# The PE work of an attention item in one place, and the state-space parameter tiles from an earlier stream by way of DRAM

## The chip, the cores and the metric

One core of one Trainium2 chip. The metric is the device time of one execution, in microseconds (us); lower is better. The engines are called as the profile calls them: PE (TensorE, matrix products and transposes), PEld (its weight loads), DVE (VectorE), ACT (ScalarE), POOL (GpSimd) and SP (SyncE, which here only issues DMAs). "Layer 0" and "layer 1" are the two layers.

## What is computed

A decoder trunk of two layers on 512 tokens of width 1024. In each layer one input projection gives ten column blocks of 512; four mixers work on them, each result is gated, and one output projection adds all four to the residual.

```python
for layer in range(DEPTH):
    proj = rms_norm(x, norm_g[layer]) @ w_in[layer]
    a_u, a_g, qd, kd, vd, b_g, c_x, c_g, m_q, m_g = jnp.split(proj, 10, axis=-1)
    y_a = s5_mixer(a_u, ...)            # A: state-space, 32 groups of 16 channels, 64 complex states
    y_b = diff_attention(q, k, v, lam)  # B: 4 heads, softmax(s1) - lam * softmax(s2), causal
    y_c = rglru_mixer(c_x, ...)         # C: convolution, then a gated linear recurrence
    y_m = memory_attention(m_q, ...)    # M: 4 heads into 256 memory tokens
    mixed = jnp.concatenate([y_a * silu(a_g), y_b * silu(b_g), y_c * silu(c_g), y_m * silu(m_g)], -1)
    x = x + mixed @ w_out[layer]
```

The state-space mixer (S5) builds from `lambda`, `log_dt`, `b` and `c` a decay `abar` and an input matrix `bb`, runs `x_t = abar * x_(t-1) + bb u_t` over the sequence and reads `c` times the state. `abar`, `bb` and all products of them with `b`, `c` and powers of `abar` depend on parameters alone, not on the tokens.

## The kernel before, in words

**Main stream.** A plan (`ORDER`) lists the projection blocks of each layer; layer 0 goes q, v, k, kv (memory keys and values), cx, au, cg, bg, mq, ag, mg, gl (the GLU of the state-space part), then four output blocks (two pairs of groups by two halves of the columns). Layer 1 goes q, k, cx, v, kv, au, mq, bg, mg, ag, cg, gl and the same output blocks. Each block reads weights in pieces of 512 KB (`raw`, 2 buffers, on SP's queue). ACT rounds a piece (`whi`, L166), DVE takes the rest (`wlo`, L172), and three matmuls (hi x hi, hi x lo, lo x hi) replace one fp32 product. `cm_block` (matmuls on L508) and `tm_block` (L528) issue 12 matmuls between two *ticks*. In the au block the stationary tiles are hidden states with a column stride of four (`h_au`).

**Side streams.** Everything else is written as Python generators that the class `Streams` steps once a tick; `yield d` means: go on after d ticks. So at each tick some attention, recurrence (lru), memory or S5 work is traced between the matmuls of the main stream. `D_AT`, `D_S5`, `D_MEM` are those distances. `st.join(name)` ticks until a stream has ended: gl joins S5, the first output block joins S5 and the memory attention, the third the rest.

**Who orders the instructions.** The tile framework takes the traced program and fills each engine's queue: program order is the priority, but an instruction goes only when its inputs and buffers are ready by the framework's own estimate, and work that is ready earlier may run ahead. Buffers of a pool are handed out in program order; most small tiles here come from one pool of nine buffers of 2 KB a partition (`b2`). Each engine's queue and each DMA queue then runs strictly in order on the chip.

**Attention** (L601 on). 16 items a layer: four query blocks i by four heads. `scores(n)` (L638 to L640) issues per map m two score matmuls (fp32r, the query's rounded part and its rest) and one bf16 matmul that adds the causal mask; then DVE and ACT do the softmax (L642 to L654) into `e`. `ptrans(n)` (L662) transposes `e` on PE in i+1 steps and ACT copies it. `av(n)` (L672) multiplies by v in fp32. One turn of the loop issues `scores(n)`, `av(n-2)`, a tick, `ptrans(n-1)`, a tick.

**S5.** `s5_params` (a stream of its own, `s5p`) makes small parameter tiles: `bbx` (input matrix), `cs_` and `cc_` (output matrix), powers `apr`, `api`, and two rotation tables `tab0`, `tab1`. For layer 0 it starts with the kernel, for layer 1 at the third output block of layer 0 (`S5P_AT = 2`). `s5` (L918 on) starts after the au block, when `s5p` has ended. It transposes the input into `U` (L923) and goes through four quarters f of the channels. In each quarter:
- W: two products and a sum on DVE, with two small ACT copies (`bby`, L941), give `wt`; a tick; PE transposes it (L948) into `WT` and multiplies it by `cs_` (L955) for `kq`; eight small POOL DMAs (L966) spread `kq` into `MT`.
- a tick; `B` = `WT` x `U` (L986); DVE makes `VV` (four products on 128x256, and four last steps on 64 partitions each, because the two halves go to different columns), then six steps on 128x512 for the rotation tables `tcq`, `tsq` from `tab0` and `tab1`, then rotates `B` into `xr`.
- a tick; eight scans (L1015), rotation back into `xp`; two ticks; `y` (L1030, L1032) = `MT` x `U` + `VV` x `xp`; a copy; two ticks.

At the end come transposes (L1044) and the GELU (L1046). `tt` (L340) is the DVE helper of all two-operand steps, so their line is L340 whatever they do. `WT`, `VV` and `MT` have one buffer each.

Of the kernel before, what the change touches and what calls it, by code (L numbers as in the profile page):

```python
# [9 lines left out]
F32 = mybir.dt.float32  # L10
# [4 lines left out]
ALU = mybir.AluOpType  # L15
# [34 lines left out]

MEM_AHEAD = 2
BD_AHEAD = 3
S5P_AT = 2
D_MEM = (3, 2, 1)
D_S5 = (1, 1, 1, 2, 2)
D_AT = (1, 1)


class Streams:
# [31 lines left out]
def tile_kernel(ctx: ExitStack, tc: tile.TileContext, A, out):  # L91
# [509 lines left out]
    def attention(l, R):  # L601
# [26 lines left out]
        def scores(n):  # L628
# [8 lines left out]
            for m in range(2):  # L637
                PE.matmul(s[:, m, :M], qh[:, m, h, :], kT[m][:, h, :M], start=True, stop=False)  # L638
                PE.matmul(s[:, m, :M], ql[:, m, h, :], kT[m][:, h, :M], start=False, stop=False)  # L639
                PE.matmul(s[:, m, i * 128:N], idb, cmb, start=False, stop=True)  # L640
            mx = ti(2, "mx")
            V.tensor_reduce(out=mx, in_=s[:, :, :N], op=ALU.max, axis=AX.X)  # L642
# [34 lines left out]
        for n in range(n_it + 2):  # L677
            if n < n_it:
                scores(n)
            if n >= 2:  # L680
                av(n - 2)
            yield D_AT[0]
            if 1 <= n <= n_it:
                ptrans(n - 1)
                yield D_AT[1]

    def attention_fin(l, R):

# [143 lines left out]
    def s5_load(l, R):  # L832
# [7 lines left out]
            nc.sync.dma_start(out=Cw[:, :, i], in_=A[n][l].rearrange("(b g) h p -> (g h) b p", b=4))  # L840
        R["B"], R["Cw"] = B, Cw

    bbx = const.tile([P, 32, 16], F32, tag="bbx", name="bbx")
    cs_ = const.tile([P, 32, 16], F32, tag="cs_", name="cs_")
    cc_ = const.tile([P, 2, 16, 16], F32, tag="cc_", name="cc_")
# [6 lines left out]
    def s5_params(l, R):  # L852
# [37 lines left out]
        for tab, size in ((tab0, 16), (tab1, 8)):  # L890
# [3 lines left out]
            while n < size:  # L894
# [13 lines left out]
                cn, sn_ = c2, s2  # L908
                yield

    def au_evac(au):
        def f(s, a):
            S.copy(au[:, :, :, T - 1 - s, :].rearrange("p q g h -> p (q g) h"), a.rearrange("p (a h) -> p a h", h=16))
        return f

    def s5(l, R):
# [11 lines left out]
        for i in range(2):  # L928
            V.memset(xp[i][:, :, 0], 0.0)
        for f in range(4):  # L930
            qs = slice(4 * f, 4 * f + 4)
            sh = [P, 8, T, 16]
            gs8 = slice(8 * f, 8 * f + 8)
            t1 = b2(sh, "wt1")
            t2 = b2(sh, "wt2")
            tt(t1, bc(apr2[:, gs8], 3, sh), bc(bbx[:, gs8], 2, sh), ALU.mult)

            bby = tiny.tile([P, 8, 16], F32, tag="bby", bufs=1, name=nm("bby"))
            for i in range(2):
                hs, ot = slice(i * 64, i * 64 + 64), slice(64 - i * 64, 128 - i * 64)  # L940
                S.activation(bby[hs], bbx[ot, gs8], AF.Copy, scale=-1.0 if i == 0 else 1.0)  # L941
            tt(t2, bc(api2[:, gs8], 3, sh), bc(bby, 2, sh), ALU.mult)
            tt(t1, t1, t2, ALU.add)
            wd = t1.rearrange("p (q g) d h -> p q (g d h)", g=2)
            yield D_S5[0]
            pt = tp()
            for j in range(4):
# [19 lines left out]
            sh = [P, 4, T, 16]  # L967
            t1 = b2(sh, "wt1")
            t2 = b2(sh, "wt2")

            def cprod(dst, x1, y1, x2, y2, op):
                tt(t1, x1, y1, ALU.mult)
                tt(t2, x2, y2, ALU.mult)
                for g in range(2):
                    hs = slice(g * 64, (g + 1) * 64)
                    tt(dst[hs, :, g], t1[hs], t2[hs], op)

            a_r = bc(apr[:, l, qs, 1:5], 3, sh)
            a_i = bc(api[:, l, qs, 1:5], 3, sh)
            c_r = bc(cc_[:, 0, qs], 2, sh)  # L980
            c_i = bc(cc_[:, 1, qs], 2, sh)
            yield D_S5[1]
            B = sc2((P, 2, 4, NC))
            for j in range(4):
                for i in range(2):
                    PE.matmul(B[:, i, j, :], WT[i][:, j].rearrange("p g c -> p (g c)"), U[:, 4 * f + j, :], start=True, stop=True)  # L986
            cprod(VV[0], a_r, c_r, a_i, c_i, ALU.add)
            cprod(VV[1], a_i, c_r, a_r, c_i, ALU.subtract)

            u1 = b2([P, 4, NC], "u1")  # L990
            u2 = b2([P, 4, NC], "u2")
            tcq = b2([P, 4, NC], "tcq")
            tsq = b2([P, 4, NC], "tsq")
            v4 = [a.rearrange("p q (a b) -> p q a b", b=16) for a in (u1, u2, tcq, tsq)]
            s4 = [P, 4, 8, 16]
            f0 = [bc(tab0[:, i, qs], 2, s4) for i in range(2)]
            f1 = [bc(tab1[:, i, qs], 3, s4) for i in range(2)]
# [104 lines left out]
    for pi, (l, n, u, ids) in enumerate(plan):  # L1102
# [37 lines left out]
        elif n == "au":  # L1140
# [182 lines left out]
```

## Time and profile before

| what | value |
| --- | --- |
| time, median of 3 executions | 924.17 us (922.41 to 924.3) |
| the profiled execution | 923.84 us, of which the span of the trace is 922.1 us |
| PE / PEld / DVE / ACT / POOL busy | 97% / 81% / 71% / 56% / 5% of the span |
| DMA | 90.59 MB, mean 98 GB/s |

The span runs from the first to the last recorded instruction. A busy share is the sum of an engine's instruction times over the span. Matmuls overlap, so a row's mean length of a matmul (0.39 us) is longer than its step in the stream; steps are read from the starts in the timeline. A wait in the trace is put down to whoever signalled last.

### The profile page before, as it was taken

How to read it: one execution, taken by the hardware profiler on the slowest of the kernel's cores; microseconds unless marked ns; L12 is line 12 of the kernel's file. 1: busy time of each engine (PE TensorE's matmuls, PEld its weight loads, DVE VectorE, ACT ScalarE, POOL GpSimd, SP SyncE). 2: the span in 40 equal slices, each digit the busy share in tenths (PEclk: the TensorE clock that was granted, in tenths of full speed). 3: DMA queues.
4: the chain of work that ended last, by engine and by line, in shares of the span. 5: the costliest groups of instructions: out<-in, count | busy, mean ns of one | idle time of the engine just before them, and what ended most of it. 6: DMA issues, size and time to landing. Idle time of an engine off the chain costs nothing.

```text
span 922.1 us, 12510 instructions
## 1 busy us (share of the span) xinstructions
PE 894.3 (97%) x4538; PEld 748.3 (81%) x4538; DVE 655.7 (71%) x1313; ACT 519.1 (56%) x1036; POOL 42.9 (5%) x94
## 2 busy tenths in 40 slices
PE   5999999999999999999999999999999999999997
PEld 4788878987887788888888888798877888788885
DVE  6985877669999946883374675964798998666343
ACT  6674776997333355831454479766646343763123
POOL 1001000001100100000100000000101110000000
PEclk9999999999999999999999999999999999999999
DMA  5833432122122226533343321432121213143322
GB/s 199 204 111 100 141 92 69 47 69 67 55 85 80 63 80 193 137 115 95 111 160 104 91 85 53 147 105 69 50 69 50 74 49 99 62 175 100 98 85 92
DMA packets 81073, 90.59 MB, mean 98 GB/s; under 512 B 23794, under 2 KB 58227, under 8 KB 81011
## 3 DMA queue, kind: packets, MB, share of 16 engines
q1 hardware_dynamic: 77986, 85.98, 30.1%
q10 hardware_dynamic: 720, 2.62, 0.9%
q0 software_dynamic: 2304, 1.18, 0.5%
q8 instruction: 36, 0.59, 0.3%
q14 instruction: 27, 0.21, 0.1%
HBM read 84.92 MB, written 4.19 MB: 97 GB/s over the span
## 4 chain that ended last, share of the span: by engine, by line
PE 70%; DVE 18%; ACT 6%; DMA 3%; issue 2%; SPq 1%; DVEq 0%; ACTq 0%
PE acc L528 36%; PE acc L508 15%; PE acc L1209 5%; DVE u L340 4%; DVE wlo L172 3%; PE tp L1032 2%; DVE xr L1015 2%; PE ms L672 1%; PE tp L826 1%; PE sc L638 1%; ACT whi L166 1%; PE tp L305 1%; PE sc L639 1%; DVE VV L340 1%; PE sc L801 1%
## 5 line engine op out<-in xcount | busy, mean ns | idle before, releaser
L166 ACT CAST whi<-raw 128x1024 fp32r<-128x1024 f32 x136 | 143.3, 1053 | 231.2 <-PE acc L528 119.8
L172 DVE TENSOR_TENSOR wlo<-raw,whi 128x1024 fp32r<-128x1024 f32 x136 | 165.9, 1220 | 115.5 <-ACT whi L166 114.7
L508 PE MATMUL acc<-hThi,whi 128*128 128x512 f32 x384 | 155.0, 404 | 0.0
L508 PE MATMUL acc<-hThi,wlo 128*128 128x512 f32 x384 | 152.8, 398 | 0.0
L508 PE MATMUL acc<-hTlo,whi 128*128 128x512 f32 x384 | 152.2, 396 | 0.0
L528 PE MATMUL acc<-whi,hThi 128*128 128x512 f32 x256 | 105.9, 414 | 0.8 <-ACT whi L166 0.8
L528 PE MATMUL acc<-wlo,hThi 128*128 128x512 f32 x256 | 101.3, 396 | 0.0
L528 PE MATMUL acc<-whi,hTlo 128*128 128x512 f32 x256 | 101.0, 395 | 0.0
L528 PE MATMUL acc<-whi,mxh 128*128 128x512 f32 x256 | 100.1, 391 | 0.0
L528 PE MATMUL acc<-whi,mxl 128*128 128x512 f32 x256 | 100.1, 391 | 0.0
L528 PE MATMUL acc<-wlo,mxh 128*128 128x512 f32 x256 | 100.1, 391 | 0.0
L508 PEld LDWEIGHTS acc<-hThi,wlo 128*128 128x128 f32 x384 | 72.7, 189 | 14.3
L508 PEld LDWEIGHTS acc<-hThi,whi 128*128 128x128 f32 x384 | 72.7, 189 | 12.9
L508 PEld LDWEIGHTS acc<-hTlo,whi 128*128 128x128 f32 x384 | 72.7, 189 | 12.9
L528 PEld LDWEIGHTS acc<-whi,hThi 128*128 128x128 f32 x256 | 56.3, 220 | 8.9 <-ACT whi L166 1.2
L528 PEld LDWEIGHTS acc<-whi,hTlo 128*128 128x128 f32 x256 | 56.1, 219 | 7.9 <-DVE hTlo L308 0.2
L528 PEld LDWEIGHTS acc<-wlo,hThi 128*128 128x128 f32 x256 | 56.7, 221 | 7.1
L528 PEld LDWEIGHTS acc<-whi,mxh 128*128 128x128 f32 x256 | 48.1, 188 | 9.8
L528 PEld LDWEIGHTS acc<-whi,mxl 128*128 128x128 f32 x256 | 48.1, 188 | 9.8
L528 PEld LDWEIGHTS acc<-wlo,mxh 128*128 128x128 f32 x256 | 48.1, 188 | 9.6
L966 POOL DMA_DIRECT2D MT<-kq x64 | 32.1, 509 | 367.8 <-DVE kq L340 230.3
L648 ACT ACTIVATE e<-sc,nmx 128x128 f32<-128x128 f32 (+3 forms) x64 | 33.3, 530 | 11.7 <-DVE nmx L644 10.2
(305 smaller groups left out, 1664.6 us busy)
## 6 DMA issues: line engine op xcount, KB each, us to landing
raw<-in_w_in_dram SPq DMA_DIRECT2D x80, 512.0 KB, 3.6
raw<-in_w_out_dram SPq DMA_DIRECT2D x32, 512.0 KB, 3.3
raw<-in_w_mem_kv_dram SPq DMA_DIRECT2D x16, 512.0 KB, 3.4
x<-in_x_dram SPq DMA_DIRECT2D x8, 512.0 KB, 5.2
raw<-in_s_w_glu_dram SPq DMA_DIRECT2D x16, 256.0 KB, 2.9
mt<-in_mem_dram SPq DMA_DIRECT2D x4, 512.0 KB
xd<-x SPq DMA_DIRECT2D x4, 512.0 KB, 4.3
x<-xd SPq DMA_DIRECT2D x4, 512.0 KB, 6.8
```

The lines of the kernel that those rows point to most:

```text
L166: S.copy(hi, wbuf[j])
L172: V.tensor_tensor(out=lo, in0=raw, in1=hi, op=ALU.subtract)
L305: lastins["pe"] = PE.transpose(pt[:, k, :], h[:, kk * 128:(kk + 1) * 128], ident)
L340: V.tensor_tensor(out=o, in0=a, in1=b, op=op)
L508: PE.matmul(a[j][:, :ncol], w[:, kk, c], h(k), start=(hf == 0 and i == 0), stop=(hf == 1 and i == 3 * nh - 1))
L528: PE.matmul(a[t], h(k, t), w[:, kk, :], start=(p == 0 and kk == 0 and i == 0), stop=(p == np_ - 1 and kk == 1 and i == 2))
L638: PE.matmul(s[:, m, :M], qh[:, m, h, :], kT[m][:, h, :M], start=True, stop=False)
L648: S.activation(e[:, m, :N], s[:, m, :N], AF.Exp, bias=nmx[:, m:m + 1], scale=0.125, accum_out=sm[:, m:m + 1])
L966: G.dma_start(out=MT[g * 64 + 64 - n:g * 64 + 64, g, t], in_=kq[g * 64:g * 64 + n])
L1015: V.tensor_tensor_scan(out=xr_[i][:, j, :], data0=dec, data1=xr_[i][:, j, :], initial=0.0, op0=ALU.mult, op1=ALU.add)
L1032: PE.matmul(y[:, j, :], xp[i][:, j, :], VV[i][:, j].rearrange("p g t h -> p (g t h)"), start=False, stop=(i == 1))
L1209: PE.matmul(a, w[:, k, s, j * 128:(j + 1) * 128], h[:, 2 * hf + k, :], start=(hf == 0 and i == 0), stop=(hf == 1 and i == 5))
```

## The change

Five edits. (1) In `scores`, both maps' score matmuls come first, then both mask matmuls. (2) A turn of the attention's loop issues `scores(n)`, `ptrans(n-1)`, `av(n-2)` one behind the other, then two ticks. (3) The W, VV and table products move from `s5` to the end of `s5_params`, each result written to DRAM by a DMA on SP, twelve steps three ticks apart. (4) `s5` reads them back: W and the two tables by SP, VV by four POOL DMAs a quarter into the two partition halves; it starts after au as soon as the first quarter is there. (5) `s5p` of layer 1 starts at the first output block of layer 0.

```diff
-S5P_AT = 2
+S5P_AT = 0
 D_S5 = (1, 1, 1, 2, 2)
-D_AT = (1, 1)
+D_S5P = 3
+D_AT = 2
...
             for m in range(2):
                 PE.matmul(s[:, m, :M], qh[:, m, h, :], kT[m][:, h, :M], start=True, stop=False)
                 PE.matmul(s[:, m, :M], ql[:, m, h, :], kT[m][:, h, :M], start=False, stop=False)
+            for m in range(2):
                 PE.matmul(s[:, m, i * 128:N], idb, cmb, start=False, stop=True)
...
             if n < n_it:
                 scores(n)
+            if 1 <= n <= n_it:
+                ptrans(n - 1)
             if n >= 2:
                 av(n - 2)
-            yield D_AT[0]
-            if 1 <= n <= n_it:
-                ptrans(n - 1)
-                yield D_AT[1]
+            yield D_AT
...
+    s5dram = ctx.enter_context(tc.tile_pool(name="s5dram", bufs=2, space=bass.MemoryType.DRAM))
...
+        R["s5d"] = []
+        for f in range(4):
+            d = {n: s5dram.tile([P, 512], F32, tag=f"{n}{f}", name=nm(f"{n}d")) for n in ("wd", "vv", "tc", "ts")}
+            w1 = b2(sh, "wp1")
+            w2 = b2(sh, "wp2")
+            tt(w1, bc(apr2[:, gs8], 3, sh), bc(bbx[:, gs8], 2, sh), ALU.mult)
...
+            tt(w2, bc(api2[:, gs8], 3, sh), bc(bby, 2, sh), ALU.mult)
+            tt(w1, w1, w2, ALU.add)
+            nc.sync.dma_start(out=d["wd"], in_=w1.rearrange("p g d h -> p (g d h)"))
+            yield D_S5P
...
+            for i, (x1, x2, op) in enumerate(((a_r, a_i, ALU.add), (a_i, a_r, ALU.subtract))):
+                tt(v1[:, i], x1, c_r, ALU.mult)
+                tt(v2[:, i], x2, c_i, ALU.mult)
+                tt(v1[:, i], v1[:, i], v2[:, i], op)
+            nc.sync.dma_start(out=d["vv"], in_=v1.rearrange("p i q t h -> p (i q t h)"))
+            yield D_S5P
...
+            for n, (i, j), (i2, j2), op in (("tc", (0, 0), (1, 1), ALU.subtract), ("ts", (1, 0), (0, 1), ALU.add)):
+                a1 = b2(s4, "tp1")
+                a2 = b2(s4, "tp2")
+                tt(a1, f0[i], f1[j], ALU.mult)
+                tt(a2, f0[i2], f1[j2], ALU.mult)
+                tt(a1, a1, a2, op)
+                nc.sync.dma_start(out=d[n], in_=a1.rearrange("p q a b -> p (q a b)"))
+            R["s5d"].append(d)
+            yield D_S5P
...
         for f in range(4):
+            while len(R["s5d"]) <= f:
+                yield
...
-            tt(t1, bc(apr2[:, gs8], 3, sh), bc(bbx[:, gs8], 2, sh), ALU.mult)
...
-            tt(t2, bc(api2[:, gs8], 3, sh), bc(bby, 2, sh), ALU.mult)
-            tt(t1, t1, t2, ALU.add)
-            wd = t1.rearrange("p (q g) d h -> p q (g d h)", g=2)
+            d = R["s5d"][f]
+            wd = b2([P, 4, 128], "wd")
+            nc.sync.dma_start(out=wd.rearrange("p q c -> p (q c)"), in_=d["wd"])
             yield D_S5[0]
...
+            vd = d["vv"].rearrange("p (i q c) -> p i q c", i=2, q=4)
+            for i in range(2):
                 for g in range(2):
                     hs = slice(g * 64, (g + 1) * 64)
-                    tt(dst[hs, :, g], t1[hs], t2[hs], op)
...
+                    G.dma_start(out=VV[i][hs, :, g].rearrange("p q t h -> p q (t h)"), in_=vd[hs, i])
+            tcq = b2([P, 4, NC], "tcq")
+            tsq = b2([P, 4, NC], "tsq")
+            nc.sync.dma_start(out=tcq.rearrange("p q c -> p (q c)"), in_=d["tc"])
+            nc.sync.dma_start(out=tsq.rearrange("p q c -> p (q c)"), in_=d["ts"])
             yield D_S5[1]
...
-            cprod(VV[0], a_r, c_r, a_i, c_i, ALU.add)
-            cprod(VV[1], a_i, c_r, a_r, c_i, ALU.subtract)
...
-            tt(v4[0], f0[0], f1[0], ALU.mult)
-            tt(v4[1], f0[1], f1[1], ALU.mult)
-            tt(v4[2], v4[0], v4[1], ALU.subtract)
-            tt(v4[0], f0[1], f1[0], ALU.mult)
-            tt(v4[1], f0[0], f1[1], ALU.mult)
-            tt(v4[3], v4[0], v4[1], ALU.add)
...
             def s5_all(l=l, R=R):
-                while "s5p" in st.live:
+                while "s5d" not in R:
                     yield
```

## Rows read from the trace of the kernel before

**Rows 1.** The page, part 1: busy time, share of the span, instructions.

```profile
PE 894.3 (97%) x4538; PEld 748.3 (81%) x4538; DVE 655.7 (71%) x1313; ACT 519.1 (56%) x1036; POOL 42.9 (5%) x94
```

**Rows 2.** Windows: stretch, length, busy PE, PEld, DVE, ACT, POOL, granted clock, DMA.

```profile
88.00:214.00 126.00, 125.36 (x684) 106.30 (x683) 94.75 (x173) 104.93 (x227) 3.47 (x9) 1.00 0.27 81
214.00:342.00 128.00, 123.06 (x648) 103.42 (x647) 113.39 (x210) 54.08 (x98) 16.05 (x32) 0.99 0.24 75
364.00:571.00 207.00, 206.64 (x981) 170.74 (x980) 128.89 (x246) 114.08 (x198) 3.93 (x10) 1.00 0.37 110
662.00:802.00 140.00, 137.23 (x757) 114.00 (x756) 120.19 (x221) 69.24 (x147) 13.96 (x28) 1.00 0.21 67
```

**Rows 3.** PE's waits, 214 to 342, then 662 to 802: total us, times, longest.

```profile
PE tp L1032 <- DVE xp L340: 1.7, 3, 0.8
PE tp L1044 <- ACT yf L1046: 1.7, 1, 1.7
PE tp L948 <- DVE wt L340: 1.5, 1, 1.5
...
PE tp L699 <- DVE bg L700: 1.2, 1, 1.2
PE tp L1032 <- DVE xp L340: 0.6, 1, 0.6
PE tp L826 <- ACT yf L1046: 0.4, 1, 0.4
PE tp L819 <- ACT yf L1046: 0.3, 1, 0.3
```

**Rows 4.** Windows around the wait at L948, columns as in rows 2.

```profile
213.50:217.00 3.50, 2.01 (x17) 1.60 (x16) 3.50 (x5) 3.25 (x9) 0.00 (x0) 0.99 0.31 109
217.00:221.00 4.00, 4.00 (x13) 3.24 (x13) 3.85 (x11) 2.63 (x5) 3.04 (x7) 0.58 0.45 137
```

**Rows 5.** Timeline of PE, one item's scores and masks: start, length, line, tiles.

```profile
159.46 0.34 PE L638 MATMUL sc<-kT,qh 128*128 128x384 f32 x1
159.63 0.34 PE L639 MATMUL sc<-kT,ql 128*128 128x384 f32 x1
159.81 0.23 PE L640 MATMUL sc<-cmb,idb 128*128 128x128 bf16 x1
159.85 0.42 PE L638 MATMUL sc<-kT,qh 128*128 128x384 f32 x1
160.11 0.33 PE L639 MATMUL sc<-kT,ql 128*128 128x384 f32 x1
```

**Rows 6.** Timeline of PE, one item's transposes in the au block.

```profile
154.66 0.49 PE L662 MATMUL tp<-cst,e 128*128 128x128 f32 x3
154.91 0.60 PE L528 MATMUL acc<-whi,hThi 128*128 128x512 f32 x1
155.35 0.40 PE L528 MATMUL acc<-wlo,hThi 128*128 128x512 f32 x1
155.59 0.40 PE L528 MATMUL acc<-whi,hTlo 128*128 128x512 f32 x1
```

**Rows 7.** Line L340 on DVE: ns min/median/max, first and last start.

```profile
L340 DVE TENSOR_TENSOR u<-tab,tab x32: 675/685/695, 219.3 to 760.1; 128x512 f32<-128x512 f32 x32
L340 DVE TENSOR_TENSOR VV<-wt,wt x32: 406/418/423, 219.9 to 757.3; 64x256 f32<-64x256 f32 x32
```

**Rows 8.** DMA issues: engine, count, KB each, median us to landing.

```profile
raw<-in_s_w_glu_dram SPq DMA_DIRECT2D x16, 256.0 KB, 2.9
...
bd<-in_lru_w_a_dram POOLq DMA_DIRECT2D x4, 64.0 KB, 2.3
```

**Rows 9.** Waits of SP's queue, 214 to 342: total us, times, longest.

```profile
SPq L152 <- DVE wlo L172: 93.1, 13, 11.2
```

**Rows 10.** Instructions that write or read bbx: ns, first and last start.

```profile
L941 ACT ACTIVATE bby<-bbx x16: 308/308/311, 50.3 to 720.6; 64x128 f32<-64x128 f32 x16
L340 DVE TENSOR_TENSOR wt<-apr,bbx x8: 672/678/689, 212.7 to 746.6; 128x512 f32<-128x512 f32 x8
```

More of the change, by code (lines that the diff above doesn't have):

```diff
@@ L909, in s5_params @@
                 yield
+        R["s5d"] = []
+        for f in range(4):
+            qs, gs8 = slice(4 * f, 4 * f + 4), slice(8 * f, 8 * f + 8)
+            d = {n: s5dram.tile([P, 512], F32, tag=f"{n}{f}", name=nm(f"{n}d")) for n in ("wd", "vv", "tc", "ts")}
+            sh = [P, 8, T, 16]
+            w1 = b2(sh, "wp1")
+            w2 = b2(sh, "wp2")
+            tt(w1, bc(apr2[:, gs8], 3, sh), bc(bbx[:, gs8], 2, sh), ALU.mult)
+            bby = tiny.tile([P, 8, 16], F32, tag="bby", bufs=1, name=nm("bby"))
+            for i in range(2):
+                hs, ot = slice(i * 64, i * 64 + 64), slice(64 - i * 64, 128 - i * 64)
+                S.activation(bby[hs], bbx[ot, gs8], AF.Copy, scale=-1.0 if i == 0 else 1.0)
+            tt(w2, bc(api2[:, gs8], 3, sh), bc(bby, 2, sh), ALU.mult)
+            tt(w1, w1, w2, ALU.add)
+            nc.sync.dma_start(out=d["wd"], in_=w1.rearrange("p g d h -> p (g d h)"))
+            yield D_S5P
+            sh = [P, 4, T, 16]
+            a_r = bc(apr[:, l, qs, 1:5], 3, sh)
+            a_i = bc(api[:, l, qs, 1:5], 3, sh)
+            c_r = bc(cc_[:, 0, qs], 2, sh)
+            c_i = bc(cc_[:, 1, qs], 2, sh)
+            v1 = b2([P, 2, 4, T, 16], "vp1")
+            v2 = b2([P, 2, 4, T, 16], "vp2")
+            for i, (x1, x2, op) in enumerate(((a_r, a_i, ALU.add), (a_i, a_r, ALU.subtract))):
[4 more added lines that the diff above has]
+            yield D_S5P
+            s4 = [P, 4, 8, 16]
+            f0 = [bc(tab0[:, i, qs], 2, s4) for i in range(2)]
+            f1 = [bc(tab1[:, i, qs], 3, s4) for i in range(2)]
+            for n, (i, j), (i2, j2), op in (("tc", (0, 0), (1, 1), ALU.subtract), ("ts", (1, 0), (0, 1), ALU.add)):
[7 more added lines that the diff above has]
+            yield D_S5P
     def au_evac(au):
@@ L930, in s5 @@
         for f in range(4):
+            while len(R["s5d"]) <= f:
+                yield
             qs = slice(4 * f, 4 * f + 4)
[L932 to L935, printed above, removed]
-            tt(t1, bc(apr2[:, gs8], 3, sh), bc(bbx[:, gs8], 2, sh), ALU.mult)
[L938 to L941, printed above, removed]
-            tt(t2, bc(api2[:, gs8], 3, sh), bc(bby, 2, sh), ALU.mult)
-            tt(t1, t1, t2, ALU.add)
-            wd = t1.rearrange("p (q g) d h -> p q (g d h)", g=2)
+            d = R["s5d"][f]
+            wd = b2([P, 4, 128], "wd")
+            nc.sync.dma_start(out=wd.rearrange("p q c -> p (q c)"), in_=d["wd"])
             yield D_S5[0]
@@ L966, in s5 @@
                     G.dma_start(out=MT[g * 64 + 64 - n:g * 64 + 64, g, t], in_=kq[g * 64:g * 64 + n])
[L967 to L973, printed above, removed]
+            vd = d["vv"].rearrange("p (i q c) -> p i q c", i=2, q=4)
+            for i in range(2):
                 for g in range(2):
                     hs = slice(g * 64, (g + 1) * 64)
-                    tt(dst[hs, :, g], t1[hs], t2[hs], op)
[L978 to L981, printed above, removed]
+                    G.dma_start(out=VV[i][hs, :, g].rearrange("p q t h -> p q (t h)"), in_=vd[hs, i])
[3 more added lines that the diff above has]
+            nc.sync.dma_start(out=tsq.rearrange("p q c -> p (q c)"), in_=d["ts"])
             yield D_S5[1]
@@ L986, in s5 @@
                     PE.matmul(B[:, i, j, :], WT[i][:, j].rearrange("p g c -> p (g c)"), U[:, 4 * f + j, :], start=True, stop=True)
-            cprod(VV[0], a_r, c_r, a_i, c_i, ALU.add)
-            cprod(VV[1], a_i, c_r, a_r, c_i, ALU.subtract)
             u1 = b2([P, 4, NC], "u1")
             u2 = b2([P, 4, NC], "u2")
[L992 to L997, printed above, removed]
-            tt(v4[0], f0[0], f1[0], ALU.mult)
-            tt(v4[1], f0[1], f1[1], ALU.mult)
-            tt(v4[2], v4[0], v4[1], ALU.subtract)
-            tt(v4[0], f0[1], f1[0], ALU.mult)
-            tt(v4[1], f0[0], f1[1], ALU.mult)
-            tt(v4[3], v4[0], v4[1], ALU.add)
             xr_ = [b2([P, 4, NC], f"xr{i}") for i in range(2)]
```

## The prediction

> **What bounds the kernel now.** I read the page first: TensorE (PE) is busy 97% of the span, VectorE (DVE) 71% [rows 1]. So the time is PE's work plus the time in which PE has none or works at a worse pace; DVE counts only where PE waits for it. The change leaves every matmul in, so all it can win are those losses. The windows view then shows where they are [rows 2]. In each row compare the stretch with PE's busy time, then look at DVE. While the attention of layer 0 runs (88 to 214 us), DVE is busy 94.75 of 126 us (75%) and PE lacks 0.64 us. While the state-space (S5) part of layer 0 runs (214 to 342), DVE is at 113.39 of 128 (89%) and PE lacks 4.94. In layer 1 (662 to 802) it is 120.19 of 140 (86%) and 2.77. From the last projections of layer 0 to the start of the next attention (364 to 571) DVE is at 62% and PE lacks 0.36.
>
> The waits view of the two S5 stretches names what PE waited for [rows 3]: the W tiles from DVE (1.5 us, L948), the decayed states xp from DVE (1.7, and 0.6 in layer 1), the gate bg from DVE (1.2), and the GELU on ScalarE (1.7). The first costs more than its length: PE is busy 2.01 of 3.5 us around it, and in the next 4 us the granted clock is 0.58, a mix of the full level, 2.4 GHz, and the half, 1.2 [rows 4]. That loses 4 x 0.42 = 1.7 us more.
>
> The last loss shows only in starts. A mask matmul (bf16) is followed by the other map's first score matmul: this takes from 159.85 to 160.11, 0.26 us, where the first map's took 0.17 from 159.46 [rows 5]. After the three transposes of an item, the next projection matmul holds PE from 154.91 to 155.35, 0.44 us, the one after it 0.24 [rows 6].
>
> **The change, part by part.**
> *Masks together.* Both masks follow both maps' scores, so a mask stands ahead of a score once less per item. A score after a mask lost 0.26 - 0.17 = 0.09 us; the mask's own slot is short, 0.04 [rows 5], so I count 0.07 net. 32 items: -2.2 us, between 0 (the scheduler pulls them apart) and -2.9 (0.09 each).
>
> *Transposes and AV behind the scores.* The 32 transpose groups lose a place of their own, and so an exit into the projection stream. One exit holds 0.20 us over the pace [rows 6], but the three transposes before it took only 0.25 (154.66 to 154.91), so part of it is their own unfinished work: I take 0.12, between the mask's 0.07 and 0.20. This exit is in the au block, whose stationary tiles are strided; I count the eight items that fall there, -1.0 us, between 0 and 32 x 0.20 = -6.4, nearer 0 because most groups stand elsewhere. Each item still takes two ticks, so the pace of the attention stays. Its transposes come one tick sooner after their scores (two, not three): where the softmax is late, the scheduler puts other matmuls between, and the grouping is lost there rather than PE.
>
> The Trainium skill has a rule against this part ("TensorE: Matmul & The Clock Gate", step-by-step section): weight loads are pulled ahead of matmuls in flight, so the next tile's load hides behind this one's matmul. Here the slot of 0.44 us after transposes against 0.24 [rows 6] says that this fails at a change of kind; by the rule the term would be zero, the third rival below.
>
> *Parameter tiles out of the S5 stretch.* Per quarter of the channels DVE did three steps for W at 0.69 us (the length of a step on a whole tile), four half-partition writes at 0.418 for VV and four products on as many elements a partition, so as long, and six steps of 0.69 for the tables [rows 7]: 2.1 + 3.3 + 4.1 = 9.5 us, 38 per layer. Without them DVE's load is 113.39 - 38 = 75 of 128 us in layer 0 and 82 of 140 in layer 1, both 59%, under the 75% of the attention's stretch, where PE lacked 0.5%. At that rate PE lacks 0.005 x 268 = 1.3 us. The GELU waits stay, 1.7 and about 0.7 in layer 1, since ScalarE makes them. So 7.7 - 1.3 - 2.4 = 4.0 us of idle time go, and the half clock with the L948 wait, 1.7: -5.7 us. Ends: 0, if the loads come as late as the products did, and -7.7 - 1.7 = -9.4.
>
> *What takes its place.* The same tiles are made once in the parameter stream, 3 + 6 + 6 products a quarter (VV's last step is now whole, so six at 0.418): 2.1 + 2.5 + 4.1 = 8.7 us, 35 per layer, with the two small ScalarE copies. Layer 1's stream starts at the first output block, in the stretch at 62%: (128.89 + 35) of 207 is 79% [rows 2], which I price at 0.5 us, between 0 and 2.5 (the layer boundary, with norm and transposes, lies in it). In layer 0 there is no such room: the steps ahead take 23 ticks and q, v and k have 24, so the twelve new steps of three ticks begin with the attention (88 us) and end some seven ticks after au, whose last tick, the 52nd, is near 214 us. So the attention's stretch holds up to 94.75 + 35 = 130 us of DVE in 126. Some spills into the S5 stretch, which now has room. PE there would lack between the 0.5% of now and the 3.9% of 214 to 342, so +0 to +4.3, and up to 1.7 of half clock: I take +1.5, nearer the low end because mostly projections fill PE there, and the attention's result is needed only by the third output block.
>
> *DMAs and queues.* Each quarter adds four writes and three reads of 256 KB on SP and four reads of 64 KB on POOL. The 256 KB loads of now land in 2.9 us, the 64 KB POOL loads of bd in 2.3 [rows 8]. The writes are read much later. VV on POOL stands behind eight small MT issues; its matmuls come four ticks on, and a tick is 12 matmuls at 0.24, 2.9 us [rows 6]: even one after another, 4 x 2.3 = 9.2 us, the loads fit in 11.6. W and the tables on SP are asked for one tick ahead of their use, just the landing time. And SP's queue is in order and sits waiting nearly always: 93.1 us in 13 waits for wlo in the S5 stretch of layer 0 [rows 9]. A load behind one comes late, and a weight load behind a write that waits for DVE does too; the latter is covered by the two spare weight pieces (24 matmuls each, 11 us in all). Price of new waits: +0.7, between 0 and the slower rival's 9.6.
>
> **Sum** against the profiled execution, 923.84 us (span 922.1): -2.2 - 1.0 - 5.7 + 0.5 + 1.5 + 0.7 = -6.2, so 917.6. That execution lies 0.3 under the median of 924.17, so I forecast 918.0 for the median. A measurement of this kernel can tell about 0.2%, 1.8 us.
>
> **The rivals.**
> 1. *Moved, not removed.* Layer 0's DVE is overfull during the attention and costs there what the S5 stretch gives back: +4.3 + 1.7 in place of +1.5, so 922.5, on the edge of no change. For it: 130 us in 126. Against: the S5 stretch at 89% lost PE time through its own short chain, which the attention has not.
> 2. *Slower: W's load comes too late.* L948 waits for the SP load as it did for DVE at 214 us. Each such case costs 1.5 + 1.7 = 3.2 us [rows 3, 4]; against a forecast 6.2 under, it decides from three of the eight quarters on; with three it gives 918.0 - 0.7 + 9.6 = 926.9. For it: SP waits 93.1 of 128 us. Against: the load is ready to go as soon as a buffer is free, and the scheduler lets ready work run ahead: the first bby copy runs at 50.3 us, its product only at 212.7 [rows 10].
> 3. *No grouping.* The scheduler parts the work again, or weights do load ahead: 918.0 + 3.2 = 921.2.
> 4. *More.* The GELU tail comes sooner and its waits go (-2.4), layer 0 has room (-1.5), half the exits beyond my eight save 0.12 (-1.4): 912.7.
>
> **How the numbers follow.** Forecast 0.43 (own range 914 to 921), rival 1 0.18, rival 2 0.15, rival 3 0.11, rival 4 0.13. Faster by over 0.2% (under 922.3) are the forecast, rivals 3 and 4 and under half of rival 1: 0.75. Within 0.2%: the rest of rival 1, 0.10. Slower (over 926.0): rival 2, 0.15. The range of 8 in 10 goes from 911.5, a little under rival 4, to 927.0, which takes in rival 2 at three quarters and leaves out more of them.
>
> **What would show it.** Right: DVE under 65% in both S5 stretches; no wait before the W transposes (L948 of before) and no dip of the clock after it; hardly a wait for xp; two masks next to each other with starts 0.04 to 0.06 us apart, then transposes and AV; 88 to 214 us over 90% DVE with PE lacking under 2 us. Wrong: the W transposes waiting for the load of wd, DVE waiting for tcq or tsq, POOL's VV releasing the y matmuls, weight casts waiting for raw loads, or the PE time of 88 to 214 us growing by what the S5 stretch sheds.

## The result: slower, and the profile after

The changed kernel takes 933.86 us (median of four runs, 930.73 to 934.83), the kernel before in the same session 923.57 (922.41 to 924.30): a ratio of 1.0111, 95% interval 1.0095 to 1.0127. I had forecast 918.0. The profiled execution is one of 934.83 us with a span of 932.9.

The page, part 1, of the changed kernel (busy time, share of the span, instructions; against [rows 1]):

```profile
PE 895.9 (96%) x4538; PEld 751.8 (81%) x4538; DVE 647.2 (69%) x1297; ACT 520.0 (56%) x1036; POOL 62.8 (7%) x126
```

The totals explain nothing. TensorE (PE) has the same matmuls and is busy 1.6 us more, VectorE (DVE) even has 8.5 us less to do; the span grew by 10.8. So PE lost time in gaps, and the question is where. The windows view, with the four stretches cut at the same projection matmuls as in [rows 2] (length, then busy PE, PEld, DVE, ACT, POOL, granted clock, DMA):

```profile
88.00:224.60 136.60, 127.74 (x676) 108.56 (x675) 117.89 (x225) 108.32 (x237) 6.40 (x14) 0.96 0.32 102
224.60:352.60 128.00, 123.81 (x655) 104.00 (x654) 84.02 (x149) 51.25 (x89) 23.57 (x44) 0.99 0.36 111
374.70:581.50 206.80, 206.33 (x980) 170.83 (x979) 155.99 (x306) 116.39 (x204) 6.38 (x14) 1.00 0.43 131
672.60:813.50 140.90, 137.58 (x763) 115.14 (x761) 91.32 (x160) 69.97 (x150) 20.50 (x38) 1.00 0.28 89
```

Read the first number after each colon pair, the length, against [rows 2]: 126 became 136.6, 128 stayed 128.0, 207 became 206.8, 140 became 140.9. **The whole loss lies in layer 0's attention**, 10.6 us, and the state-space (S5) stretches gained next to nothing, though DVE's share there fell from 89% to 66% and from 86% to 65%. (The border between these two stretches is good to 1 us: the attention's last AV, eight matmuls, stands before it in the kernel before and behind it in all others whose stretches are compared here. The two together grew by 10.6.) The load went where I said it would go, and the time did not follow it. In the first row DVE is busy 118 of 137 us: 86%, less than I had feared, and yet PE lacks 8.9 us and the clock is at 0.96.

PE's waits in 88 to 228, in the S5 part of layer 0 (228 to 356) and in 672 to 813 (total us, times, longest; against [rows 3]):

```profile
PE sc L639 <- ACT e L650: 5.5, 2, 4.2
PE sc L640 <- DVE ql L341: 1.7, 1, 1.7
...
PE tp L1049 <- DVE xp L341: 3.8, 4, 1.9
PE tp L985 <- DMA wd<-wdd: 0.4, 1, 0.4
...
PE tp L1049 <- DVE xp L341: 2.1, 3, 1.1
```

New are the scores that wait for an exp (they need the score buffer that the exp still reads) and for ql. In S5 the waits for the W tile (L948 of before) and for the gate went, as I had counted on, and so did the GELU wait of layer 0, which I hadn't; but the waits for xp grew from 1.7 to 3.8 us and from 0.6 to 2.1. (Part of both is the attention's edits: e1 below has neither the W wait nor the gate's, and waits 2.3 and 1.6 us for xp.) Around the long wait for the exp, two windows of the same columns:

```profile
189.50:194.00 4.50, 0.42 (x4) 0.23 (x3) 3.04 (x6) 4.43 (x12) 0.00 (x0) 0.77 0.13 48
194.00:198.00 4.00, 3.92 (x15) 3.21 (x16) 2.77 (x5) 4.00 (x8) 0.00 (x0) 0.50 0.03 11
```

PE stands for 4.2 us, and in the four that follow the granted clock is 0.50, its half level of 1.2 GHz: some 2 us more. ScalarE (ACT) is full here (4.43 of 4.50). The scores that this exp belongs to were issued at 184.8 to 188.5 us; before the change the same item's ran at 170.1 to 172.4. So the attention came 14.7 us later and 40 projection matmuls further down the stream (620 of them stand before these scores, 580 before the change), into the stretch where ACT has the recurrence's sigmoids. What put it behind stands at 106 to 119 us. ACT's timeline there (start, length, line, tiles):

```profile
106.35 0.37 ACT L675 ACTIVATE qT<-ms,rc 128x128 f32<-128x128 f32 x1
...
112.24 0.62 ACT L624 CAST qh<-qT 64x512 fp32r<-64x512 f32 x1
112.89 2.01 ACT L167 CAST whi<-raw 128x1024 fp32r<-128x1024 f32 x2
114.79 0.26 ACT L666 COPY pT<-tp 128x128 f32<-128x128 f32 x1
114.95 0.37 ACT L677 ACTIVATE jk<-ms,rc 128x128 f32<-128x128 f32 x1
```

The first row is the evacuation of an AV, the last the square of the same AV, which could follow at once and comes 8.6 us later. The pT in between copies transposes that PE made at 105.6. And DVE's timeline just beside it:

```profile
111.67 1.88 DVE L341 TENSOR_TENSOR tp<-tab,tab 128x512 f32<-128x512 f32 x3
113.48 0.68 DVE L341 TENSOR_TENSOR tp<-tp,tp 128x512 f32<-128x512 f32 x1
...
116.12 0.16 DVE L653 RECIPROCAL rc<-sm 128x2 f32<-128x2 f32 x1
```

The softmax of the third item had its exps by 106.4 us; its reciprocal comes at 116.1, behind table products ("tp" here is the product of L341, not the PSUM tile). Two theories fit. The products fill DVE and stand ahead of the softmax; or the products take buffers that pT and the square need, so that the order of the queues puts these late, and with them the reciprocal: its result `rc` has two buffers, and the square of two items before must first free one. A third showed in SP's queue, 88 to 228 us:

```profile
SPq L153 <- DVE wlo L173: 47.2, 13, 7.2
SPq L952 <- DVE tp L341: 28.4, 6, 13.3
SPq L928 <- DVE wp L341: 18.9, 2, 13.5
```

The writes to DRAM wait up to 13.5 us for their product, with weight loads queued behind them.

One prediction is seen at once. PE's timeline of one item's last score and both masks, against [rows 5]:

```profile
106.98 0.28 PE L640 MATMUL sc<-kT,ql 128*128 128x256 f32 x1
107.10 0.29 PE L642 MATMUL sc<-cmb,idb 128*128 128x128 bf16 x2
107.19 0.48 PE L529 MATMUL acc<-whi,mhi 128*128 128x512 f32 x1
```

Both masks are over in 0.09 us, and no score follows a mask any more.

### The profile page after: what moved, and what is told of

The parts are those of the page before. It is cut to its first block, busy times and chain, and to the rows that moved or that the text cites. A ratio compares the mean times of both kernels' runs of the same rounds, so it can differ in the third digit from the quotient of the medians.

```text
span 932.9 us, 12684 instructions
## 1 busy us (share of the span) xinstructions
PE 895.9 (96%) x4538; PEld 751.8 (81%) x4538; DVE 647.2 (69%) x1297; ACT 520.0 (56%) x1036; POOL 62.8 (7%) x126
## 4 chain that ended last, share of the span: by engine, by line
PE 67%; DVE 16%; ACT 6%; DMA 5%; issue 4%; POOL 1%; SPq 1%; DVEq 0%; ACTq 0%; POOLq 0%
PE acc L529 33%; PE acc L509 16%; PE acc L1226 5%; DVE wlo L173 2%; DVE u L341 2%; DVE xr L1032 2%; PE tp L1049 2%; ACT whi L167 1%; DMA MT<-kq 1%; PE sc L802 1%; PE tp L827 1%; DVE tp L341 1%; PE ms L674 1%; PE tp L306 1%; PE sc L639 1%
## 5 line engine op out<-in xcount | busy, mean ns | idle before, releaser
L529 PE MATMUL acc<-whi,hThi 128*128 128x512 f32 x256 | 104.0, 406 | 0.8 <-ACT whi L167 0.8
L509 PEld LDWEIGHTS acc<-hThi,whi 128*128 128x128 f32 x384 | 72.8, 189 | 13.5 <-ACT whi L167 0.4
```

Of the source, the lines that this page charges most:

```text
L509: PE.matmul(a[j][:, :ncol], w[:, kk, c], h(k), start=(hf == 0 and i == 0), stop=(hf == 1 and i == 3 * nh - 1))
L529: PE.matmul(a[t], h(k, t), w[:, kk, :], start=(p == 0 and kk == 0 and i == 0), stop=(p == np_ - 1 and kk == 1 and i == 2))
```

## The experiments

The theories: **A**, DVE overfull (my rival 1); **B**, weight loads behind waiting writes on SP; **C**, the attention's own new order; **D**, the pool b2 of nine 2 KB buffers runs out. Ratios are against the kernel before on the same chip; between runs on different chips a difference in us is good to about 1, as the kernel before itself had medians from 922.95 to 923.98.

**The two halves apart.** e1 is the kernel before with the attention's edits, e2 the changed kernel without them, e3 the kernel before with the first of them alone, e4 the changed kernel with the square's tile moved:

```
-                PE.matmul(s[:, m, i * 128:N], idb, cmb, start=False, stop=True)      # e1, e3; undone in e2
+            for m in range(2):
+                PE.matmul(s[:, m, i * 128:N], idb, cmb, start=False, stop=True)
...
+            if 1 <= n <= n_it:                       # e1; undone in e2
+                ptrans(n - 1)
             if n >= 2:
                 av(n - 2)
-            yield D_AT[0]
-            if 1 <= n <= n_it:
-                ptrans(n - 1)
-                yield D_AT[1]
+            yield D_AT
...
-            jk = b2([P, 128], "jk")                  # e4
+            jk = tiny.tile([P, 128], F32, tag="ajk", name=nm("jk"))
```

> The kernel before with the attention's two edits alone (masks behind both maps' scores; transposes and AV behind the scores); the state-space part makes its own tiles as before. Kernel before 923.6, changed 933.9. Theory A (VectorE is overfull during layer 0's attention), theory B (weight loads stand behind writes that wait for VectorE on SP) and theory D (the nine b2 buffers run out because of the new products) all need the products in the attention, so they expect no loss here: 919 to 923, my -3.2 of the prediction. Theory C (the new order of the attention itself stalls TensorE, since scores, transposes and AV stand in a row with nothing between) expects most of the loss here: 929 or more, with scores that wait for the exp around 190 us.

Measured 920.92 us, ratio 0.9973 (0.9962 to 0.9985). Faster; theory C, taken by itself, falls.

> The changed kernel with the attention's emission as before (mask after each map's scores, transposes a tick after the scores); parameter tiles by way of DRAM as in the change. Theories A, B and D expect the loss to stay: 931 to 937 (the changed 933.9 plus the 0 to 3 that the attention's edits had saved). Theory C expects it to go: 918 to 925.

Measured 927.46, ratio 1.0042 (1.0027 to 1.0057). The way over DRAM alone loses 4 us, not 10: less than A, B or D had said. The halves (-2.4 and +4.2) make +1.8, the whole +10.3; 8.5 us are interaction: the new order costs nothing by itself, but with the products in the attention it does.

> The kernel before with the masks behind both maps' scores and nothing else. My step of -2.2 expects 921.4 (between 920.7 and 923.6). If the mask's place between the maps costs nothing that a later start doesn't cost too, 923.6 within 0.5. All of A to D expect no loss; a loss over 1 would put part of it on the masks.

Measured 921.90, ratio 0.9986 (0.9976 to 0.9995): -1.4, so the mask's place does cost something, if less than I had it.

> The changed kernel with the square of the attention's AV (only its sum is used) written to a small tile of its own and no longer to one of the nine b2 buffers. Theory D expects the softmax chain no longer to wait for a b2 buffer: 925 to 929, at least 5 of the 10 us given back, and the attention to finish its items earlier than in the changed kernel. Theories A, B and C expect 933 within 1.5.

Measured 929.16, ratio 1.0063 (1.0048 to 1.0078). A junk tile of 512 bytes a partition taken out of b2 gives back 4.7 us. That speaks for D, and its timeline shows how (ACT):

```profile
106.48 0.37 ACT L675 ACTIVATE qT<-ms,rc 128x128 f32<-128x128 f32 x1
106.73 0.38 ACT L677 ACTIVATE jk<-ms,rc 128x128 f32<-128x128 f32 x1
...
115.07 0.41 ACT L666 COPY pT<-tp 128x128 f32<-128x128 f32 x2
```

The square now follows its AV at once. pT, which still needs a b2 buffer, is as late as before. Two windows of the changed kernel, then of e4, show that the loss has two places and which of them came back:

```profile
110.00:132.00 22.00, 18.49 (x80) 13.68 (x79) 20.25 (x40) 13.59 (x36) 0.00 (x0) 0.92 0.44 142
176.00:198.00 22.00, 17.72 (x82) 15.33 (x82) 15.41 (x26) 21.74 (x39) 0.00 (x0) 0.86 0.10 37
...
110.00:132.00 22.00, 18.41 (x82) 13.94 (x82) 20.26 (x39) 13.56 (x36) 0.00 (x0) 0.92 0.46 151
176.00:198.00 22.00, 20.46 (x100) 17.52 (x100) 15.64 (x28) 21.44 (x46) 0.00 (x0) 1.00 0.22 70
```

At 110 to 132 us PE lacks 3.5 us in the one and 3.6 in the other; at 176 to 198 it lacks 4.3 in the changed kernel, with the granted clock at 0.86, and 1.5 in e4 at 1.00. e2, with the old order, has the same two figures at 3.0 and 0.6, and its pT too comes late (116.23 us, behind two weight casts). So the first loss goes with the late pT; the second, the long wait for the exp, came only where the new order and the square in b2 met. Why the new order needs more of b2 isn't shown.

**One suspect each.** e5 keeps the way over DRAM for layer 1 only:

```
         R["s5d"] = []
+        if l == 0:
+            return
...
+            own = l == 0
+            if own:
...
```

(where "own" is set, the S5 part makes its tiles as before). e6 sends layer 0's products to POOL, e7 sends the writes from POOL's queue, e8 changes the S5 part's pauses (the edits in short):

```
-                tt(w1, ...)                          # e6, all products of s5_params
+                (G if l == 0 else V).tensor_tensor(out=w1, ...)
-            nc.sync.dma_start(out=d["wd"], ...)      # e7, all four writes
+            G.dma_start(out=d["wd"], ...)
-D_S5 = (1, 1, 1, 2, 2)                               # e8
+D_S5 = (1, 1, 1, 3, 1)
```

> The changed kernel with the way over DRAM in layer 1 only; layer 0 makes its tiles in its state-space part as before; the attention's edits stay. The loss was found in layer 0's attention, so this should come out under the kernel before: 919 to 922, that is the 920.9 of the attention's edits alone, less what layer 1's state-space stretch gains (0 to 1.5) plus up to 1 for the products in the output blocks. If layer 1 loses something too, 923 or more. The prediction's step of -5.7 for both layers would make it about 918.

Measured 920.07, ratio 0.9968 (0.9955 to 0.9981). Layer 1 loses nothing; what it gains over e1 (0.9 us by the times, 0.5 by the ratios) is inside the intervals.

> The changed kernel with layer 0's products (15 a quarter) computed by POOL in place of VectorE; same buffers, same writes to DRAM, same order of the streams. Theory A (VectorE overfull, the products stand ahead of ql, of rc and of the W casts) expects most of the loss to go: 921 to 926. Theory D (b2 buffers run out) expects it to stay or grow, since a slower engine holds the buffers longer: 933 to 940. Theory B (weight loads behind waiting writes on SP) expects the same, as the writes wait longer still: 933 to 940.

Measured 937.32, ratio 1.0151 (1.0134 to 1.0168). With DVE rid of the products the loss grew, as D and B had it and A not. This isn't clean: POOL and DVE slow each other (last section). PE's waits over the span show the attention as the victim again:

```profile
PE tp L664 <- DVE e L656: 5.2, 6, 1.8
PE sc L639 <- ACT e L650: 3.2, 5, 1.9
```

> The changed kernel with the sixteen writes a layer issued from POOL's queue in place of SP's. Theory B expects weight loads no longer to stand behind writes that wait for VectorE: 926 to 930, with raw pieces 29 to 31 issued in an even rhythm around 190 us. Theories A and D expect 932 to 935, no difference that counts.

Measured 934.56, ratio 1.0126 (1.0111 to 1.0141): no gain. PE's two largest waits in 88 to 228 us are those of the changed kernel, to the digit (5.5 in 2 for the exp, 1.7 for ql). Theory B falls.

> The changed kernel with the state-space part's y matmuls three ticks (not two) after the scans, and the next quarter's load one tick (not two) after them, so that a quarter stays eight ticks. The waits for xp (5.9 us in 7 in the changed kernel, 2.3 in 4 before) did not go with VectorE's load. If they are the length of the chain from B to xp against three ticks of cover, they go: 928 to 931. If VectorE's load or the loads of tcq and tsq make them, or if the wait only moves to W, 933 within 1.5.

Measured 930.85, ratio 1.0085 (1.0070 to 1.0100): 3.0 less than the changed kernel, as expected. (A quarter is seven ticks in both, not eight as I wrote.)

**The pool itself.** e9 leaves all of the change in place and only moves the product tiles out of b2, into one of the fourteen 8 KB buffers; e10 does the opposite to e1, with no products in the attention:

```
-            w1 = b2(sh, "wp1")                       # e9; v1, v2, a1, a2 alike
-            w2 = b2(sh, "wp2")
+            pb = b8([P, 4, 512], "pp")
+            w1, w2 = (pb[:, k].rearrange("p (g d h) -> p g d h", g=8, d=T) for k in range(2))
...
-    sm2 = ctx.enter_context(tc.tile_pool(name="sm2", bufs=9))      # e10
+    sm2 = ctx.enter_context(tc.tile_pool(name="sm2", bufs=8))
```

e11 is e5, and e12 is e9, each with the pauses of e8.

> The changed kernel with the products of a quarter in one 8 KB tile of the pool of fourteen large buffers, so that none of the six product tiles takes one of the nine b2 buffers; VectorE's work, the writes and the streams stay. Theory D (b2 runs out: pT and the AV's square get their buffer late, so softmax chain and attention fall behind) expects 922 to 927, with the pT copy of the second item near 110 us in place of 114.8 and the scores of item i3 h0 near 172 us in place of 184.8. Theory A (VectorE overfull) expects 932 to 935. If the large buffers run out in their turn, the S5 part or the gates wait for one instead: above 928 with a wait for them.

Measured 921.90, ratio 0.9982 (0.9972 to 0.9992): 12 us less than the changed kernel, and faster than the kernel before. The windows of the four stretches, cut as above, then ACT's timeline:

```profile
88.20:215.10 126.90, 123.54 (x676) 106.06 (x675) 115.18 (x219) 105.48 (x234) 3.80 (x11) 1.00 0.32 104
215.10:339.80 124.70, 122.03 (x656) 102.71 (x655) 79.35 (x140) 50.79 (x88) 23.63 (x44) 1.00 0.34 111
361.80:568.90 207.10, 206.75 (x980) 170.65 (x980) 157.16 (x306) 116.14 (x204) 6.37 (x14) 1.00 0.42 131
659.70:800.00 140.30, 137.46 (x762) 115.06 (x761) 91.32 (x160) 69.92 (x150) 20.57 (x38) 1.00 0.28 89
```

```profile
111.40 0.27 ACT L666 COPY pT<-tp 128x128 f32<-128x128 f32 x1
111.57 0.37 ACT L677 ACTIVATE jk<-ms,rc 128x128 f32<-128x128 f32 x1
...
113.34 1.99 ACT L167 CAST whi<-raw 128x1024 fp32r<-128x1024 f32 x2
```

The attention's stretch fell from 136.6 to 126.9 us with nearly as much for DVE to do in it: DVE is busy 91% of it, more densely than the 86% of the slower kernel, and PE lacks 3.4 where it lacked 8.9. What differs is the order: pT stands ahead of the weight casts again. The item at 184.8 us now has its scores at 176.9 (I had said 172). Theory D is shown in this: with the same work for every engine, the place of the product tiles makes the loss; A is not its cause. (The one large tile also makes the products of a quarter wait for each other in another way than eight small ones did; e4, which leaves the products alone, speaks for the pool by itself.)

> The attention's edits alone (920.9) with eight b2 buffers in place of nine and no products in the attention at all. Theory D expects that the pool alone makes a loss: 924 or more, in the stretch of 88 to 214 us. Theory A expects at most 1: 921 to 922.

Measured 931.26, ratio 1.0084 (1.0069 to 1.0100). One buffer less costs 10.3 us over e1, without one product in the attention: the pool is at its limit already. But the loss isn't where I said. Cut at the same matmuls, 88 to 214 stays at 123.7 us, the S5 stretch of layer 0 takes 130.1 (e1: 126.5), the start of layer 1's attention, 571 to 662 in the kernel before, 95.1 (e1: 91.3), and the S5 stretch of layer 1 142.8 (e1: 140.7). The first two, whole:

```profile
212.40:342.50 130.10, 122.80 (x658) 102.97 (x656) 112.09 (x208) 54.23 (x102) 16.10 (x32) 1.00 0.23 72
571.70:666.80 95.10, 90.89 (x504) 80.23 (x503) 64.68 (x120) 64.22 (x155) 3.47 (x7) 0.96 0.28 87
```

> The best so far (DRAM in layer 1 only, attention's edits; 920.1) with the y matmuls one tick later. In the changed kernel that saved 3.0, in both state-space parts. The chain from B to xp is the same in both ways of making the tiles, so 916.5 to 918.5; if the waits for xp of layer 0 are the load of the products there, only layer 1 gains: 918.5 to 919.5.

Measured 919.80, ratio 0.9959 (0.9944 to 0.9974): 0.3 under e5 (0.9 by the ratios, as the chips differ), less than the first line had it and inside the intervals. The waits for xp fell from 4.3 us to 3.0.

> The changed kernel with both: products in a large buffer and y one tick later. If the two causes are separate, e9 less 3: with theory D 919 to 924, with theory A 929 to 932.

Measured 920.50, ratio 0.9967 (0.9958 to 0.9977): 1.4 under e9. The later y gives less where PE waited less for xp.

**What was still open.** e13 is e9 with as many products again (some run twice, some three times in place of a sum; a repeated one writes the same values), e14 is e1 with the square's own tile, e15 the kernel before with the pauses of e8, e16 is e12 with the square's own tile.

```
+            for _ in range(2):                       # e13; fifteen products more a quarter in all
+                tt(w1, bc(apr2[:, gs8], 3, sh), bc(bbx[:, gs8], 2, sh), ALU.mult)
```

> The kernel with the products in a large buffer (e9, 921.9) with every product of the parameter stream computed twice, so that VectorE has 35 us more per layer in the places where it had them already, and nothing else. This prices VectorE's load by itself. Theory A's price (some 0.1 to 0.3 us of TensorE per us of VectorE in a full stretch) expects 926 to 933. If VectorE's load hardly counts and the buffers were all of it, 922 to 924.

Measured 950.21, ratio 1.0297 (1.0281 to 1.0312): 28 us over e9. The stretch of layer 0's attention took 153.8 us, 27 more than in e9, while the output stretch with layer 1's doubled products took 209.6, 2.5 more. Two windows, the whole stretch and its worst part, then PE's waits in 88 to 243:

```profile
88.20:242.00 153.80, 134.19 (x689) 113.57 (x688) 142.36 (x279) 108.09 (x239) 6.39 (x14) 0.92 0.31 102
184.00:224.00 40.00, 26.40 (x105) 20.27 (x105) 36.77 (x69) 35.57 (x72) 0.00 (x0) 0.74 0.19 66
```

```profile
PE sc L639 <- ACT e L650: 11.2, 5, 4.9
```

So A's mechanism exists. From e1 to e9 the stretch took on 17.6 us of DVE work (97.56 to 115.18) and grew by 3.1; the next 27.2 (to 142.36) cost 26.9. e9 stands just under an edge.

> The attention's edits alone (920.9) with the AV's square in a small tile of its own, so that b2 has more room and there are no products. Theory D, if the pool binds in the kernel before as well, expects 918 to 920; if it binds only with the products in it, 920.9 within 0.6.

Measured 920.36, ratio 0.9969 (0.9957 to 0.9981). Against e1 within what can be told, and the attention's stretch takes 123.8 us in both: the pool doesn't bind in layer 0's attention without the products.

> The kernel before with the y matmuls one tick later and nothing of the change. My step of -5.7 took the waits for xp for VectorE's load; the state-space stretches gained nothing once the products were out of them. If the waits are the length of the chain from B to xp against its cover of ticks, a tick more helps here as well: 921 to 922.5. If not, 923.5 within 0.7.

Measured 923.25, ratio 1.0004 (0.9994 to 1.0014): nothing. A tick more for the chain does not shorten the waits for xp before the change (2.5 us in 4, against 2.3 in 4).

> The whole change with both pool remedies (products in a large buffer, the AV's square in its own tile) and y one tick later. Over e12 (920.5) the square out of b2 should take the late softmax of the last items (a 2.0 us wait of the transposes at 211 us): 917 to 919.5. If that wait is VectorE's load, 920 to 921.

Measured 922.88, ratio 0.9994 (0.9985 to 1.0003): 2.4 worse than e12, against all I expected. PE's waits in 88 to 218:

```profile
PE sc L639 <- ACT e L650: 2.4, 2, 2.2
PE tp L664 <- DVE e L656: 1.7, 1, 1.7
```

The wait at the attention's end (1.9 in e9, 1.7 here) stays, and a score that waits 2.2 us for an exp came to it. I take it that one tile more in another pool gave all queues another order, with a gap that the other hadn't; no run separates that. An order made anew is worth some 2 us either way here.

**The best sum.** e17 is e5 with the square's own tile, e18 that and the later y.

> A candidate for the best: the attention's edits, the way over DRAM in layer 1 only, and the AV's square out of b2. From 920.1 (e5) less the 0.6 that the square alone brought on the attention's edits (e14): 919.5, between 918.5 and 921. The stall of 2.4 us that a new order of the softmax brought in e16 is the danger: then 922.

Measured 920.38, ratio 0.9970 (0.9959 to 0.9981).

> The same with y one tick later. In the kernel before that tick brought nothing (e15), in the changed kernel 3.0 and with the large buffer 1.4: 918 to 919.5, and not under 917.

Measured 919.30, ratio 0.9961 (0.9947 to 0.9974). The later y brought 1.1 over e17. e11 and e18 are the fastest, some 4 us under the kernel before; their intervals overlap, and most of the gain (2.4) is the attention's edits alone.

## Why the prediction was wrong

*What bounds the kernel* held: the loss is PE's gaps, and DVE's total is no guide (8.5 us less of it, 10 us slower).

*Masks, -2.2:* -1.4 (e3), within its bounds. Right in mechanism.

*Transposes and AV, -1.0:* e1 less e3 is 921.90 - 920.92 = -1.0. With the masks -2.4 of my -3.2. That isn't noise (e1's seven runs all lie under e3's ten), but the number is partly luck: with e1 the W wait (1.5 us and the half clock behind it) and the gate's (1.1) went, which I had booked under the next term, while the waits for xp (2.3 to 3.9) and for the softmax's `e` (0.7 to 1.9) grew. Only 4 of 32 transpose groups are followed by a projection matmul in e1, 28 in e3, so the grouping came about; what the saved exits alone brought no run separates. The Trainium skill's rule against it ("TensorE: Matmul & The Clock Gate", step-by-step section), that the next weight load hides behind the matmul in flight, would have made that part zero. These runs don't settle it.

*Parameter tiles out of S5, -5.7:* the second failure. Without the pool's trouble, e9 against e1, the S5 stretches went from 126.5 to 124.7 and from 140.7 to 140.3: -2.2. The windows of e1, cut at the same matmuls (layer 0's attention, its S5, layer 1's S5):

```profile
88.20:212.00 123.80, 122.14 (x675) 105.62 (x674) 97.56 (x174) 102.66 (x221) 2.95 (x8) 1.00 0.28 84
212.00:338.50 126.50, 122.52 (x657) 103.00 (x656) 111.06 (x208) 54.96 (x102) 16.04 (x32) 1.00 0.24 74
659.00:799.70 140.70, 137.99 (x762) 114.65 (x761) 121.28 (x225) 71.31 (x154) 12.56 (x26) 1.00 0.22 68
```

I let the waits for xp go with DVE's load, as the rate of 0.5% at 75% load was to hold here. They didn't: 3.9 us in 7 in e1, 4.4 in 7 in e9. The W wait and the gate's were gone in e1 already, so the moved tiles had nothing left to win there; what went with them was a GELU wait of 1.7, which I had expected to stay. I then took xp for the length of a chain. e8, e12 and e18 agree (a tick later, 3.0, 1.4 and 1.1 us came back), e15 doesn't (nothing) and e11 tells little: what sets those waits is not settled.

*Layer 1's products in the output blocks, +0.5:* 207.1 us in e9 and in e1: 0.

*New DMA waits, +0.7:* the W transposes waited 0.4 and 0.2 us for the load. Rival 2 did not happen; the writes on SP's queue, behind which weight loads stood, cost nothing that e7 got back.

*Layer 0's attention, +1.5:* **the step that failed.** I wrote that the stretch "holds up to 94.75 + 35 = 130 us of DVE in 126" and priced it by DVE's share. By that resource the price was 3.1 (e9 against e1: 126.9 against 123.8), inside my range of 0 to 4.3. But the step moved more than DVE's time. It takes eight buffers a quarter from b2 (two for W, two for VV, two for each table), the same nine that pT and the square of the attention use, and the gate blocks of the recurrence (two bd, two bh, two bl) stand in b2 at just that time: all six around 111 us, and bh and bl, four of the nine, until their matmuls at 168 to 188. In the S5 stretch of layer 0 the same products began as the attention ended (the first W product at 212.7 us [rows 10], the last AV at 212.8). The change paid 136.6 - 126.9 = 9.7 us there for buffers, and 12.0 over the whole kernel (933.9 against 921.9); so the stretch's 126 became 126 - 2.2 (the attention's edits, 1 of it the border) + 3.1 + 9.7 = 136.6. The prediction costs instructions, DMAs and queues of the moved step, and none of the buffers that its tiles hold; b2 does not occur in it. The 12.0 holds with the attention's new order; with the old one the way over DRAM lost 4.2 in all (e2), and how much of that is buffers was not tried.

*The rivals:* rival 1 had the right place (layer 0's attention gives back what S5 saves), priced at 4.3 + 1.7 = 6.0, where the stretch lost 136.6 - 123.8 = 12.8 against e1, and mostly for another reason. Against it I had that the attention has no short chain of its own; it has one, from the scores through the exp back to the one score buffer (5.5 us of waits). With the pool relieved the change came out at 921.9, near its 922.5, and there by its own mechanism, though both terms were about half of what it had, or less: +3.1 in the attention against -2.2 in S5. That the sum fits is luck.

One link was argued, not shown: that the queues' order puts pT behind the casts because, when the order was made, its buffer was thought to come free only then. The runs show that the place of the tiles decides. A tenth b2 buffer was not tried.

## What to carry to other kernels

When work is moved to another stage, list what it holds as well as what it runs: each tile's pool, who else draws on that pool in the new stage, and what is queued behind an allocation that comes late. A moved temporary in a shared pool can cost more than its instructions, and moving it to another pool is a test of a few lines that should come before any argument about engine load. Doubling the moved work is the other cheap test: it shows how far the stage is from the point where more work costs its full length.

## What the runs showed of the hardware

A product of 128x512 on POOL beside VectorE, from e6. POOL's own rows (mean ns after the busy time) and a row of DVE's timeline:

```profile
L916 POOL TENSOR_TENSOR tp<-tab,tab 128x512 f32<-128x512 f32 x16 | 20.3, 1288 | 25.3 <-DVE li L746 10.7 <-PE tp L734 6.1 <-PE ms L674 4.5
L916 POOL TENSOR_TENSOR tp<-tp,tp 128x512 f32<-128x512 f32 x8 | 12.5, 1557 | 0.4
```

```profile
113.34 2.33 DVE L173 TENSOR_TENSOR wlo<-raw,whi 128x1024 fp32r<-128x1024 f32 x1
```

Beside DVE, POOL needs 1.29 to 1.56 us for what DVE does in 0.69 [rows 7]; the shortest took 1.05. And the wlo cast at 113.34, which starts while POOL runs a product from 113.28 to 114.59, takes 2.33 us, against a mean of 1.22 in the changed kernel: moving a product to the idle engine slowed the busy one. 1.25 us of POOL's product were still to run, and the cast took 1.11 longer. Nine such casts of this trace ran beside a POOL product for over 0.1 us: seven took 1.36 to 2.33 us and two 1.21; the 127 others took 1.20 to 1.23. The Trainium skill ("SBUF — State Buffer", section "Who interferes with whom") says that a DVE instruction with two SBUF inputs contends with a GpSimd one that reads SBUF, for a read interface that they share; the seven casts agree, the two don't show it.

Tiles that came back from DRAM took longer to land than the rows by which I had costed them [rows 8]: 4.1 us for 256 KB against 2.9 for the glu loads, 3.1 for POOL's 64 KB against 2.3. The writes took 2.0 to 4.2. PE felt 0.6 us of it.

```profile
wdd<-wp SPq DMA_DIRECT2D x8, 256.0 KB, 2.0
vvd<-vp SPq DMA_DIRECT2D x8, 256.0 KB, 4.2
VV<-vvd POOLq DMA_DIRECT2D x32, 64.0 KB, 3.1
...
wd<-wdd SPq DMA_DIRECT2D x8, 256.0 KB, 4.1
```
